# A two-layer decoder trunk in split fp32: the second part of each weight chunk formed by ScalarE and an accumulating transfer

## The chip, the cores and the metric

The kernel runs on one core of a Trainium2 chip. The metric is the device time of one execution in microseconds (us), as the median of several runs. A trace of one profiled execution shows the engines: TensorE (PE, with its weight loads as PEld), VectorE (DVE), ScalarE (ACT), GpSimd (POOL) and the DMA queues of SyncE (SP), ScalarE and GpSimd.

## The reference, cut to what matters

The reference is a decoder trunk of two layers on 512 tokens of width 1024, with 256 memory tokens. What matters here is that nearly all its work is matrix products with weights that are used once:

```python
z = h @ w_in                               # mixers of both layers
return jnp.concatenate([y_a, y_b], axis=-1) @ w_out
q = (h @ w_q).reshape(...)                 # cross-attention, 256 memory tokens
k, v = jnp.split(mem_n @ w_kv, 2, axis=-1)
return o.reshape(b, s, D_MODEL) @ w_o
return jnp.square(jax.nn.relu(h @ w_up)) @ w_down     # MLP, 1024 -> 4096 -> 1024
```

The mixers are a gated linear recurrence beside forgetting attention (layer 0) and dilated beside sliding-window attention (layer 1). Inputs and outputs are fp32.

## The kernel before

Each fp32 operand of a product is split into two parts of the type fp32r: a first part `hi`, the value rounded by ScalarE's copy, and a second part `lo = value - hi`. `mm3` then makes three matmuls of each pair, first part by first part, first by second, and second by first (lines 177, 178 and 179), which add up in one PSUM bank.

Weights come in chunks of 128 x 1024 fp32 (512 KB). There are 246 of them that `chunk` brings in; the first weights of all are loaded apart, in two halves, as `wr_first`. A chunk needs three tiles: `raw` (tag `wr`, **two** buffers), `h` (tag `wh`, three buffers) and `lo` (tag `wl`, three buffers). SyncE loads `raw`, ScalarE writes `h` from it (line 156), VectorE writes `lo` as `raw - h` (line 157). In most stages a chunk then feeds 24 matmuls of 512 columns; a chunk of the cross-attention's key projections feeds 24 of 256 columns.

The order of instructions is the order in which Python emits them, changed by the framework's priorities: `chunk` raises the priority of its instructions by 100, so they stand well ahead of the matmuls that use them in each engine's queue, as far as the buffers allow. Each engine works through its own queue strictly in order; semaphores tie them together. In the mixers, `merge` interleaves the steps of the attention heads with those of the projections by estimated costs and due times.

Names that come up: `kv` and `acth` are work tiles of the MLP (lines 908 and 920: ScalarE takes relu of a PSUM bank and squares it); `rope_raw` in the second layer's mixer sends four transfers of 64 KB per rotated projection through SyncE's queue (line 1009), which swap halves of a tile `kv` inside SBUF; `Stats.add` with `sq=G` has GpSimd square the eight input tiles at the start (line 260); GpSimd also scales the softmax's rows (`p`, line 348). GpSimd issues no transfer in this kernel.

Of the kernel before, what the change touches and what calls it, by code (L numbers as in the profile page):

```python
# [9 lines left out]
F32 = mybir.dt.float32  # L10
F32R = mybir.dt.float32r
BF16 = mybir.dt.bfloat16
AF = mybir.ActivationFunctionType
ALU = mybir.AluOpType
# [22 lines left out]
def build(ctx, tc, a):  # L37
    nc = tc.nc
    V, A, G, T, SY = nc.vector, nc.scalar, nc.gpsimd, nc.tensor, nc.sync
# [113 lines left out]
    def hi_lo(hi, lo, src, scale=None):  # L153

        if scale is None:
            A.activation(out=hi, in_=src, func=AF.Copy)  # L156
            V.tensor_tensor(out=lo, in0=src, in1=hi.bitcast(F32), op=ALU.subtract)  # L157
        else:
            A.activation(out=hi, in_=src, func=AF.Copy, scale=scale)
            V.scalar_tensor_tensor(out=lo, in0=src, scalar=scale, in1=hi.bitcast(F32),  # L160
                                   op0=ALU.mult, op1=ALU.subtract)

    def chunk(src):

        cnt[0] += 1
        i = cnt[0]
        started.append(i)
        with tc.high_priority(100 if len(started) > 4 else 0):
            raw = wp.tile([128, 1024], F32, tag="wr", name=f"wr_{i}", bufs=2)
            h = wp.tile([128, 1024], F32R, tag="wh", name=f"wh_{i}", bufs=3)  # L170
            lo = wp.tile([128, 1024], F32R, tag="wl", name=f"wl_{i}", bufs=3)
            SY.dma_start(out=raw, in_=src)
            hi_lo(h, lo, raw)
        return h, lo

    def mm3(ps, wh, wl, xh, xl, start, stop):
# [4 lines left out]
    def proj(src, xs, after, n=S, ks=range(8), need=(), give=(), bank=None):  # L181


        st = {}

        def f(k):
            def g():
                if not st:
                    st["ps"] = (bank or pmm)()[:, :n]
                    st["w"] = [c.rearrange("p (k m) -> p k m", k=8) for c in (src if type(src) is tuple else chunk(src))]  # L190
                h, lo = st["w"]
                mm3(st["ps"], h[:, k, :], lo[:, k, :], xs[k][0], xs[k][1], k == ks[0], k == ks[-1])
                if k == ks[-1]:
                    after(st["ps"])
            return g

        return [step(0.65 * n / S, f(k), need[k] if len(need) == 8 else need if k == ks[0] else (), give if k == ks[-1] else ()) for k in ks]

    def proj2(src, xs, k0, afters, need=(), banks=None):

        st = {}

        def f(e, k):
            def g():
                if "w" not in st:
                    st["w"] = [c.rearrange("p (e k m) -> p e k m", e=2, k=4) for c in chunk(src)]
                if k == 0:
                    st[e] = (banks[e] if banks else pmm)()
                h, lo = st["w"]
                x = xs[k0 + k]  # L210
                mm3(st[e], h[:, e, k, :], lo[:, e, k, :], x[0], x[1], k == 0, k == 3)
                if k == 3:
                    afters[e](st[e])
            return g

        return [step(0.65, f(e, k), need[k] if need else ()) for e in range(2) for k in range(4)]

    def proj_v(srcs, xs, out, nb, store, give=()):

        st = {}  # L220

        def f(kk, k2):
            def g():
                if not st:
                    st["ps"] = [pmm() for _ in range(min(nb, 3))] + [psc() for _ in range(nb - 3)]
                if k2 == 0:
                    st["w"] = [c.rearrange("p (k m) -> p k m", k=2) for c in chunk(srcs[kk])]
                h, lo = st["w"]
                k = 2 * kk + k2
                for b in range(nb):  # L230
                    c = slice(b * 128, (b + 1) * 128)
                    xh, xl = xs[k][0][:, c], xs[k][1][:, c]
                    T.matmul(st["ps"][b], lhsT=xh, rhs=h[:, k2, :], start=k == 0, stop=False)  # L233
                    T.matmul(st["ps"][b], lhsT=xh, rhs=lo[:, k2, :], start=False, stop=False)  # L234
                    T.matmul(st["ps"][b], lhsT=xl, rhs=h[:, k2, :], start=False, stop=k == 7)  # L235
                if k == 7:
                    for b in range(nb):
                        out.append(store(b, st["ps"][b]))
            return g

        return [step(0.65 * nb, f(kk, k2), (), give if (kk, k2) == (3, 1) else ()) for kk in range(4) for k2 in range(2)]
# [1018 lines left out]
```

## Time and profile before

| what | value |
|---|---|
| median of 3 runs | 1474.03 us (1473.45 to 1474.35) |
| the profiled execution's own time | 1476.31 us |
| span of that execution, from the first to the last instruction | 1474.4 us |
| PE busy | 1441.2 us, 98% of the span |
| DVE busy | 880.9 us, 60% |
| ACT busy | 670.9 us, 45% |
| POOL busy | 162.2 us, 11% |
| chunks formed by `chunk` | 246 |

The busy time of PE is that of overlapping matmuls, so 98% says that PE hardly ever waited, and not that it ran at its peak. The other engines have idle time, which costs nothing as long as what PE needs next is there in time. The difference of 1.9 us between the profiled execution's time and its span lies before the first and after the last instruction.

### The profile page before, as it was taken

Reading aid. Unit: us, or ns where it says so; the run is one execution under the profiler, and the core shown is the slowest. Engines: PE = TensorE matmul, PEld = TensorE weight load, DVE = VectorE, ACT = ScalarE, POOL = GpSimd, SP = SyncE. Lnnn points to the kernel's source line nnn. Section 1 sums busy time; section 2 is a strip of 40 time slices with the busy share of each in tenths; the row PEclk is TensorE's granted clock in tenths of the full one; section 3 lists DMA queues with packets and bytes.
Section 4 is the critical chain, followed back from the end, with each engine's and each line's share of the span. In section 5 each row is a group of like instructions: output and inputs, shape, how many; then the busy total and the mean of one; then the engine's idle time right before and its main releaser. Section 6 shows DMA issues by size and latency. Waiting matters only on the chain.

```text
span 1474.4 us, 18320 instructions
## 1 busy us (share of the span) xinstructions
PE 1441.2 (98%) x6912; PEld 1195.4 (81%) x6912; DVE 880.9 (60%) x1525; ACT 670.9 (45%) x1161; POOL 162.2 (11%) x172
## 2 busy tenths in 40 slices
PE   8999999999999999999999999999999999999996
PEld 5777887888888888888888788788888888888885
DVE  7788876645444444444578989765554444444543
ACT  4777764544431423224457867544444223232342
POOL 3003221001200000000213312300020000000012
PEclk9999999999999999999999999999999999999998
DMA  5222224432233323333332222343333333333331
GB/s 191 83 86 81 78 65 142 133 93 90 86 100 97 94 96 100 100 95 91 100 107 80 79 79 79 100 128 114 88 93 93 99 94 94 100 101 92 96 99 57
DMA packets 46327, 142.83 MB, mean 97 GB/s; under 512 B 5792, under 2 KB 11296, under 8 KB 46240
## 3 DMA queue, kind: packets, MB, share of 16 engines
q1 hardware_dynamic: 45152, 140.63, 31.9%
q8 instruction: 54, 0.88, 0.2%
q10 hardware_dynamic: 1088, 1.05, 0.2%
q14 instruction: 33, 0.27, 0.1%
HBM read 136.15 MB, written 2.10 MB: 94 GB/s over the span
## 4 chain that ended last, share of the span: by engine, by line
PE 84%; DVE 8%; ACT 4%; issue 1%; DMA 1%; SPq 0%; POOL 0%; DVEq 0%; ACTq 0%; POOLq 0%
PE mm L178 24%; PE mm L177 24%; PE mm L179 24%; DVE wl L157 2%; PE t L354 1%; ACT wh L156 1%; PE s L177 1%; PE s L178 1%; PE s L179 1%; PE mm L234 1%; PE mm L233 1%; PE mm L235 1%; DVE hgl L160 1%; PE pv L446 1%; PE s L422 1%
## 5 line engine op out<-in xcount | busy, mean ns | idle before, releaser
L156 ACT ACTIVATE wh<-wr 128x1024 fp32r<-128x1024 f32 x246 | 260.2, 1059 | 560.3 <-PE mm L178 508.2
L157 DVE TENSOR_TENSOR wl<-wr,wh 128x1024 fp32r<-128x1024 f32 x246 | 302.6, 1231 | 245.5 <-ACT wh L156 238.2
L177 PE MATMUL mm<-hgh,wh 128*128 128x512 f32 x888 | 350.7, 395 | 0.9 <-DVE qkl L576 0.7
L178 PE MATMUL mm<-hgl,wh 128*128 128x512 f32 x888 | 347.8, 392 | 3.7 <-DVE hgl L160 3.7
L179 PE MATMUL mm<-hgh,wl 128*128 128x512 f32 x888 | 347.1, 391 | 0.0
L177 PE MATMUL mm<-acth,wh 128*128 128x512 f32 x504 | 197.8, 395 | 0.8 <-DVE hT L474 0.8
L178 PEld LDWEIGHTS mm<-hgl,wh 128*128 128x128 f32 x888 | 167.4, 189 | 36.4 <-DVE hgl L160 4.4
L178 PE MATMUL mm<-actl,wh 128*128 128x512 f32 x504 | 196.7, 390 | 0.1
L179 PE MATMUL mm<-acth,wl 128*128 128x512 f32 x504 | 196.7, 390 | 0.0
L177 PEld LDWEIGHTS mm<-hgh,wh 128*128 128x128 f32 x888 | 167.3, 188 | 34.4 <-DVE qkl L576 1.1
L179 PEld LDWEIGHTS mm<-hgh,wl 128*128 128x128 f32 x888 | 167.2, 188 | 33.9
L270 POOL TENSOR_TENSOR ssq<-ssq,sq 128x512 f32<-128x512 f32 (+1 forms) x48 | 72.4, 1508 | 984.3 <-ACT sq L258 983.9
L934 DVE TENSOR_TENSOR kv<-mm,Rt 128x512 f32<-128x512 f32 x56 | 38.7, 692 | 150.8 <-PE mm L179 150.8
L177 PEld LDWEIGHTS mm<-acth,wh 128*128 128x128 f32 x504 | 94.4, 188 | 20.8 <-ACT acth L156 1.4
L179 PEld LDWEIGHTS mm<-acth,wl 128*128 128x128 f32 x504 | 94.6, 188 | 19.5
L178 PEld LDWEIGHTS mm<-actl,wh 128*128 128x128 f32 x504 | 94.7, 188 | 19.1 <-DVE actl L157 0.7
L348 POOL TENSOR_SCALAR p<-p,den 128x256 f32<-128x256 f32 (+1 forms) x96 | 65.7, 689 | 255.5 <-DVE den L347 186.2
L177 PE MATMUL mm<-v,wh 128*128 128x256 f32 (+1 forms) x260 | 87.0, 335 | 0.0
L178 PE MATMUL mm<-v,wh 128*128 128x256 f32 (+1 forms) x260 | 86.9, 334 | 0.0
L179 PE MATMUL mm<-v,wl 128*128 128x256 f32 (+1 forms) x260 | 86.8, 334 | 0.0
L474 DVE TENSOR_TENSOR hT<-hT,mm 128x512 f32<-128x512 f32 x53 | 35.8, 682 | 52.5 <-PE mm L179 52.4
L157 DVE TENSOR_TENSOR ptl<-t,pth 128x128 fp32r<-128x128 f32 (+3 forms) x112 | 53.2, 482 | 10.0 <-ACT pth L156 9.5
(293 smaller groups left out, 2110.8 us busy)
## 6 DMA issues: line engine op xcount, KB each, us to landing
wr<-in_mlp_up SPq DMA_DIRECT2D x64, 512.0 KB, 3.6
wr<-in_mlp_down SPq DMA_DIRECT2D x64, 512.0 KB, 3.6
wr<-in_cd_w_in SPq DMA_DIRECT2D x18, 512.0 KB, 3.7
wr<-in_xa_q SPq DMA_DIRECT2D x16, 512.0 KB, 3.7
wr<-in_xa_k SPq DMA_DIRECT2D x16, 512.0 KB, 3.7
wr<-in_xa_v SPq DMA_DIRECT2D x16, 512.0 KB, 3.7
wr<-in_xa_w_o SPq DMA_DIRECT2D x16, 512.0 KB, 3.6
wr<-in_ab_w_in SPq DMA_DIRECT2D x15, 512.0 KB, 3.6
```

The lines of the kernel that those rows point to most:

```text
L156: A.activation(out=hi, in_=src, func=AF.Copy)
L157: V.tensor_tensor(out=lo, in0=src, in1=hi.bitcast(F32), op=ALU.subtract)
L160: V.scalar_tensor_tensor(out=lo, in0=src, scalar=scale, in1=hi.bitcast(F32), op0=ALU.mult, op1=ALU.subtract)
L177: T.matmul(ps, lhsT=wh, rhs=xh, start=start, stop=False)
L178: T.matmul(ps, lhsT=wh, rhs=xl, start=False, stop=False)
L179: T.matmul(ps, lhsT=wl, rhs=xh, start=False, stop=stop)
L233: T.matmul(st["ps"][b], lhsT=xh, rhs=h[:, k2, :], start=k == 0, stop=False)
L234: T.matmul(st["ps"][b], lhsT=xh, rhs=lo[:, k2, :], start=False, stop=False)
L270: eng.tensor_tensor(out=self.ssq, in0=self.ssq, in1=q, op=ALU.add)
L348: G.tensor_scalar(out=p, in0=p, scalar1=dens[:, i:i + 1], scalar2=1.0, op0=ALU.mult, op1=ALU.mult)
L474: V.tensor_tensor(out=hT[:, e, :], in0=hT[:, e, :], in1=ps, op=ALU.add)
L934: V.tensor_tensor(out=t, in0=ps, in1=Rt, op=ALU.mult)
```

## The change

In `chunk` the call of `hi_lo` is replaced by three instructions. ScalarE writes `h` as before. ScalarE then writes `-h` into `lo`. GpSimd then issues a transfer of `raw` onto `lo` with an adding operation, so that `lo` ends as `raw - h`. VectorE has no part in it any more. All other splits (`hi_lo` of activations, of the statistics and of `wr_first`) are as before. Tiles and their numbers of buffers are as before.

```diff
@@ -170,7 +170,9 @@
             h = wp.tile([128, 1024], F32R, tag="wh", name=f"wh_{i}", bufs=3)
             lo = wp.tile([128, 1024], F32R, tag="wl", name=f"wl_{i}", bufs=3)
             SY.dma_start(out=raw, in_=src)
-            hi_lo(h, lo, raw)
+            A.activation(out=h, in_=raw, func=AF.Copy)
+            A.activation(out=lo, in_=h.bitcast(F32), func=AF.Copy, scale=-1.0)
+            G.dma_start(out=lo, in_=raw, accum_op=ALU.add)
```

The lines below the change move down by two. The order in which the instructions stand on an engine is shown at three places.

ScalarE's queue in the MLP's up-projection, before: the copy of a chunk (`wh`), then relu (line 908) and square (line 920) of an earlier chunk's result.

```order
L156 ACTIVATE wh_4984<-wr_4983 128x1024
L908 ACTIVATE kv_4899<-mm_4868 128x512
L920 ACTIVATE acth_4901<-kv_4899 128x512
L156 ACTIVATE wh_5022<-wr_5021 128x1024
L908 ACTIVATE kv_4937<-mm_4906 128x512
L920 ACTIVATE acth_4939<-kv_4937 128x512
```

The same queue and place with the change (lines 910 and 922 are relu and square now):

```order
L173 ACTIVATE wh_5157<-wr_5156 128x1024
L910 ACTIVATE kv_5070<-mm_5038 128x512
L174 ACTIVATE wl_5158<-wh_5157 128x1024
L922 ACTIVATE acth_5072<-kv_5070 128x512
L173 ACTIVATE wh_5196<-wr_5195 128x1024
L910 ACTIVATE kv_5109<-mm_5077 128x512
```

The negation stands behind the relu of an earlier chunk, so one 128x512 instruction lies between a chunk's copy and its negation.

GpSimd's queue at the start of the program, before: the squares of the input tiles, then the first `rstd`. The brackets name what an instruction waits for.

```order
L260 TENSOR_TENSOR sq_6_221<-hT 128x512 [waits DMAHW2_49,DVE_49]
L260 TENSOR_TENSOR sq_7_224<-hT 128x512 [waits DMAHW3_49,DVE_49]
L298 TENSOR_TENSOR rstd_343<-sm_341,half_neg 128x4 [waits DVE_49]
L348 TENSOR_SCALAR p_962<-p_962,den_963 128x512 [waits DMAHW7_49,DVE_49]
L348 TENSOR_SCALAR p_962<-p_962,den_963 128x384 [waits DVE_49]
```

The same with the change (the squares are at line 262):

```order
L262 TENSOR_TENSOR sq_6_222<-hT 128x512 [waits DMAHW2_49,DVE_49]
L262 TENSOR_TENSOR sq_7_225<-hT 128x512 [waits DMAHW3_49,DVE_49]
L175 DMA wl_140<-wr_138 128x1024 [waits DMAHW5_49,Activation_49]
L175 DMA wl_260<-wr_258 128x1024 [waits DMAHW6_49,Activation_49]
L175 DMA wl_350<-wr_348 128x1024 [waits DMAHW5_49,PE_49,Activation_49]
```

The adding transfers of the first chunks stand behind the last square, and each waits for its load and for ScalarE.

SyncE's queue in the second layer's mixer, before: the swaps of one projection (line 1009), then loads of weight chunks, which wait for VectorE to have read a raw buffer.

```order
L1009 DMA kv_6192<-kv_6190 32x512 [waits DMAHW5_49]
L172 DMA wr_6432<-in_cd_w_in 128x1024 [waits DMAHW6_49,DVE_49]
L172 DMA wr_6533<-in_cd_w_in 128x1024 [waits DMAHW7_49,DMAHW1_49,DVE_49]
L1009 DMA kv_6263<-kv_6261 32x512 [waits DMAHW0_49,Activation_49]
L1009 DMA kv_6263<-kv_6261 32x512
```

The same with the change; `DMASW` is the completion of a transfer that GpSimd issued:

```order
L1011 DMA kv_6318<-kv_6316 32x512 [waits DMAHW5_49]
L172 DMA wr_6562<-in_cd_w_in 128x1024 [waits DMAHW6_49,DMASW0_49]
L172 DMA wr_6664<-in_cd_w_in 128x1024 [waits DMAHW1_49,DMAHW7_49,DMASW1_49,Activation_49]
L1011 DMA kv_6391<-kv_6389 32x512 [waits DMAHW0_49,DVE_49,Activation_49]
L1011 DMA kv_6391<-kv_6389 32x512
```

The place of the loads among the swaps is the same; each load now waits for an adding transfer to have landed.

## Rows read from the trace of the kernel before

**Rows 1.** The page: busy time by engine, transfers by queue, the two groups replaced.

```profile
PE 1441.2 (98%) x6912; PEld 1195.4 (81%) x6912; DVE 880.9 (60%) x1525; ACT 670.9 (45%) x1161; POOL 162.2 (11%) x172
...
q1 hardware_dynamic: 45152, 140.63, 31.9%
...
L156 ACT ACTIVATE wh<-wr 128x1024 fp32r<-128x1024 f32 x246 | 260.2, 1059 | 560.3 <-PE mm L178 508.2
L157 DVE TENSOR_TENSOR wl<-wr,wh 128x1024 fp32r<-128x1024 f32 x246 | 302.6, 1231 | 245.5 <-ACT wh L156 238.2
```

**Rows 2.** Waits, PE only: waiter, releaser, us in total, times, longest.

```profile
PE mm L177 <- ACT wh_first L156: 5.8, 1, 5.8
PE mm L178 <- DVE hgl L160: 5.0, 3, 2.1
...
PE pv L445 <- DVE kv L395: 0.5, 1, 0.5
PE t L354 <- DVE v L157: 0.4, 1, 0.4
```

**Rows 3.** Timeline, MLP of layer 0, ACT, DVE and SP: start, length, instruction, idle before.

```profile
566.28 1.06 ACT L156 ACTIVATE wh<-wr 128x1024 fp32r<-128x1024 f32 x1 [4.38 <-PE mm L178]
567.25 0.58 ACT L908 ACTIVATE kv<-mm 128x512 f32<-128x512 f32 x1
...
571.72 1.06 ACT L156 ACTIVATE wh<-wr 128x1024 fp32r<-128x1024 f32 x1 [3.23 <-PE mm L178]
...
567.37 1.23 DVE L157 TENSOR_TENSOR wl<-wr,wh 128x1024 fp32r<-128x1024 f32 x1 [3.75 <-ACT wh L156]
...
568.63 0.33 SPq L172 DMA_DIRECT2D wr<-in_mlp_up  x1
```

**Rows 4.** Issues of transfers: size, median us from issue to landing.

```profile
wr<-in_mlp_up SPq DMA_DIRECT2D x64, 512.0 KB, 3.6
...
kv<-kv SPq DMA_DIRECT2D x52, 64.0 KB, 2.0
```

**Rows 5.** Line 172 (the loads) from 262 to 268 us, two loads.

```profile
DMA to landing us min/median/max: 3.5/4.1/4.7
```

**Rows 6.** Stretches; DVE and ACT instructions that read `wr` only (count = chunks).

```profile
core 0: us, DVE busy (x) ACT busy (x), PEclk, DMA share, GB/s
13.00:95.00 82.00, 17.93 (x15) 15.75 (x15) 1.00 0.35 107
95.00:207.00 112.00, 15.73 (x13) 12.62 (x12) 1.00 0.24 74
207.00:293.00 86.00, 24.62 (x20) 21.11 (x20) 0.98 0.42 127
293.00:352.00 59.00, 9.97 (x9) 8.48 (x8) 1.00 0.28 83
352.00:743.00 391.00, 89.15 (x73) 77.38 (x73) 1.00 0.32 97
743.00:933.10 190.10, 25.71 (x22) 23.28 (x22) 1.00 0.28 80
933.10:1016.00 82.90, 25.36 (x20) 20.04 (x19) 1.00 0.45 134
1074.00:1441.00 367.00, 83.08 (x68) 72.26 (x69) 1.00 0.32 96
```

**Rows 7.** Timeline at the start, POOL and DVE.

```profile
22.25 1.96 POOL L260 TENSOR_TENSOR sq<-hT 128x512 f32<-128x512 f32 x1 [0.63 <-DVE ssq L270]
...
19.52 1.21 DVE L157 TENSOR_TENSOR wl<-wr,wh 128x1024 fp32r<-128x1024 f32 x1
```

**Rows 8.** Waits, DVE only, from 743 to 932 us.

```profile
DVE kv L1015 <- DMA kv<-kv: 3.7, 2, 3.2
```

**Rows 9.** The end: a stretch (PEclk after the engines), and PE's timeline.

```profile
1462.00:1474.00 12.00, 2.50 (x10) 2.07 (x9) 5.66 (x13) 0.89 (x2) 3.02 (x4) 0.53 0.51 175
...
1459.36 0.71 PE L308 MATMUL t<-ident,rstd 128*128 128x128 f32 x4 [0.45 <-POOL rstd L298]
1465.76 1.23 PE L308 MATMUL t<-ident,rstd 128*128 128x128 f32 x4 [1.14 <-POOL rstd L298]
```

## The prediction, made before the change was run

> **What bounds the kernel now.** I read the page first: PE is busy 98% of the span, DVE 60%, ACT 45%, POOL 11% [rows 1]. The waits of PE are the next view. There are 18 rows of them, from 5.8 us down to 0.2 us, 25 us in all; twelve name DVE, from 5.0 us to 0.4 us, and these add up to 14.5 us [rows 2]. So what DVE is relieved of can give back 14.5 us at most, and the kernel is bound by PE.
>
> Then the cadence of a chunk. In the MLP, ACT's copy of one chunk starts at 566.28 and of the next at 571.72 us: PE uses up a chunk in 5.44 us, and ACT's copy has idled 4.38 us until PE released a `wh` buffer [rows 3]. Over the program, 508 of the 560 us that ACT idled before these copies ended with PE [rows 1]. The weights therefore come ahead of PE, and the question is how much room there is.
>
> The room is that of the two raw buffers. A raw buffer goes round so: SyncE issues the load, 0.03 us after DVE has read the chunk before (567.37 + 1.23 = 568.60, issue at 568.63); the load lands 3.6 us later; ACT copies it (1.06 us); DVE subtracts (1.23 us) [rows 3, 4]. That is 5.9 us of work; with two buffers a chunk could come every 3.0 us. PE wants one every 5.44 us, so today the loop has 2 x 5.44 = 10.88 us for 5.9 us of work.
>
> **The change part by part.** It takes 246 DVE instructions of 1.231 us away, 302.6 us [rows 1]. DVE is not the bound; of this at most the 14.5 us above come back, and only where DVE is late for another reason than a chunk. I count nothing.
>
> It adds 246 negations on ACT. The trace has none; the nearest row is the copy of the same shape, 1.06 us [rows 3], so between nothing and 1.06 us, and I take 1.06. ACT goes from 671 to some 930 us busy, 63% of the old span [rows 1]. That hides in ACT's 560 us of idle time before the copies; but the negation lies inside the loop of the raw buffer. In the MLP's up-projection a relu of 0.58 us stands between copy and negation (the order above); that is half of the MLP's chunks, so 0.3 us on average.
>
> It adds 246 transfers from SBUF to SBUF that read `raw` and `lo` and write `lo`. The load of the next chunk waits for their landing, and so do the matmuls of line 179. Call the time from the negation's end to the landing D. No row shows an adding transfer, nor any transfer that GpSimd issues. Two rows give a plain transfer: 64 KB inside SBUF lands after 2.0 us, 512 KB from HBM after 3.6 us [rows 4]. A line through them is 1.77 us fixed and 1.83 us per 512 KB. From below, D is 3.6 us, if reading the second operand costs nothing. The middle: two operands are read, 1.77 + 2 x 1.83 = 5.4 us. On top comes the load that runs beside it: the loads keep the 16 DMA engines 31.9% of 1474.4 us for 140.63 MB, which is 268 times 512 KB: 1.75 us per chunk [rows 1]; half of this is 0.9 us. GpSimd makes these transfers in place of SyncE's queue, at a cost between nothing and the 2 us that one of its squares takes; SyncE's own issue, which is part of the landing times above, takes 0.33 us [rows 3, 7], and nearer to that I take 0.5. So D = 5.4 + 0.9 + 0.5 = 6.8 us. From above, if the adding halves the rate of the whole transfer: 2 x 5.4 = 10.8 us. I take the middle because the second read is certain and the halving is not.
>
> The load has the adding transfer beside it too. Two loads that met other traffic landed after 3.5 and 4.7 us, 4.1 on average [rows 5]; I take 4.2 for all.
>
> One round of a raw buffer is then 0.03 + 4.2 + 1.06 + 0.3 + 1.06 + 6.8 + 0.05 (handing over) = 13.5 us, and a chunk comes every **6.75 us**, where PE wants 5.44. All but D is 6.7 us of it, so the room is used up at D = 10.88 - 6.7 = 4.2 us, or at 4.8 us if the loads keep their 3.6.
>
> The sum goes by stretches [rows 6]: the number of chunks times 6.75 us, less the length of the stretch, where that is positive. 13 to 95 us: 15 x 6.75 - 82 = 19. 207 to 293 (cross-attention of layer 0): 135 - 86 = 49. 352 to 743 (MLP): 493 - 391 = 102. 933 to 1016 (cross-attention of layer 1): 128 - 83 = 45. 1074 to 1441 (MLP): 466 - 367 = 99. The mixers' attention (12 chunks in 112 us, 22 in 190) and the output projections (8 in 59, and another such stretch of 58 us) need a chunk every 7.3 us or less often: nothing. Together **314 us**.
>
> Two more terms. At the start, GpSimd's queue holds the squares ahead of the first adding transfer; the last ends at 22.25 + 1.96 = 24.2 us, and D later is 31.0, where DVE had the first `wl` ready at 19.52 + 1.21 = 20.7 [rows 7]: **10 us**. In the second mixer the swaps stand behind loads that wait in SyncE's queue, now for a landing that comes up to 6.8 + 1.06 - 1.23 = 6.6 us later. There are 13 sets of swaps, so between nothing and 86 us; DVE had waited for a swap only twice, 3.7 us in all [rows 8], so they come with time in hand, and I take a quarter, **21 us**. GpSimd's row scaling stands behind adding transfers that wait for ACT. There a chunk is needed every 8 to 9 us only [rows 6], so its load and copy are long done; I count nothing, and if the cover failed, 34 chunks at one negation each, 36 us.
>
> The sum is 314 + 10 + 21 = 345 us on the profiled execution's 1476.3 us: 1821 us. The median of the runs is 2.3 us below that execution, so I predict **1819 us**.
>
> **A rule against it.** The Trainium skill, "DMA: Bandwidth & Descriptors", in its section on the anatomy of a DMA by the GpSimd path, puts such a transfer at about 2.0 us plus its bytes over 436 GB/s. For 512 KB that is an estimate of 3.2 us, with D below the bound at which the loop breaks. By it a chunk would come every 4.65 us, and the sum would be 13 us in the two cross-attention stretches, 7 at the start and 10 for the swaps: some 1504 us. No row here shows this path. The same skill, "Collectives: The Full Stack", in its part on why ReduceScatter is half of AllGather, says that the adding in a transfer costs no time of its own, but that two reads halve the rate; that is the middle value above, from another side.
>
> **The rivals.**
> *The adding transfer is hidden.* With D = 3.6 and loads at 3.6 us a round is 9.7 us, 4.85 per chunk, less than 5.44. Only the cross-attention stretches are denser: 20 x 4.85 - 86 = 11 and 19 x 4.85 - 83 = 9. With 7 at the start and 11 for the swaps: 1512 us. For it: plain transfers of this size [rows 4]. Against: it reads a second operand.
> *The adding is slow.* D = 10.8: 8.75 us per chunk. The sums over all stretches are 732 us, with 14 and 35 beside them: 2255 us. Against it: nothing in the trace; for it: nothing either, it is the upper bound.
> *The clock falls.* At the end, where PE was busy 2.5 of 12 us, the granted clock was 0.53, near the lower of its two levels, 1.2 of 2.4 GHz, and four matmuls took 1.23 us in place of 0.71 [rows 9]. If that met half of the 196 chunks of the stretches that lengthen, each would take 5.44 x 1.73 = 9.4 us: 98 x 2.65 = 260 us more, 2079 us. Against it: PE would still be busy 5.44 of every 6.75 us, far more than at the end.
> *It gets faster.* If D is below 2.8 us, the densest stretch (4.3 us per chunk [rows 6]) is covered too (0.03 + 3.6 + 1.06 + 1.06 + 2.8 + 0.05 = 8.6), and what is left is DVE's relief: 1476.3 + 5.5 at the start - 14.5, or 1465 us in terms of the median. It takes an adding transfer of 512 KB that lands hardly later than a plain one of 64 KB (2.0 us).
>
> **How the numbers follow.** The forecast has a chance of 0.53; its own range, D from 5.4 to 8.4 us, is 1677 to 1988 us by the same sums (6.05 and 7.55 us per chunk). Hidden 0.14, slow adding 0.21, clock 0.08, faster 0.03; 0.01 is left. The range of 1500 to 2160 us takes in the hidden case, the forecast, the clock, and slow adding up to D = 10 us; it leaves out the rest of slow adding and the faster case. All but the last two hundredths or so of these end slower than before by more than 0.2%, about what a measurement of this kernel can tell from no change: faster 0.03, same 0.02, slower 0.95.
>
> **What would show it.** In the profile after, ACT's `wh` waits for the load and no longer for PE; PE waits for the adding transfers' `wl` or for `wh`, in each chunk of the MLP and not in the mixers' attention; the landing of GpSimd's transfers gives D, and the distance of two copies in the MLP gives half a round. DVE falls by some 300 us and ACT rises by some 260. Wrong would be: copies still 5.44 us apart (hidden); a distance near 6.75 but a much longer mixer (queues, not the loop); a granted clock near 0.5 over the MLP; or a D whose length is GpSimd's own issuing time and not the transfer.

## The result, and the profile after

The changed kernel takes 1759.17 us (median; 1743.68 to 1781.21 us over four runs), against 1474.19 us before in the same comparison: a ratio of 1.190, with an interval of 1.182 to 1.197. That is 285 us slower, where 345 were forecast, and inside the range. One of the four runs, the one of 1781.21 us, counts as slow and is not in the ratio; the median of the other three is 1758.37 us.

The page of the changed kernel answers to [rows 1]: busy time by engine, the two groups that now form the second part, the transfers by queue (`q0` is GpSimd's).

```profile
PE 1543.7 (88%) x6912; PEld 1233.7 (70%) x6912; DVE 612.7 (35%) x1279; ACT 900.3 (51%) x1405; POOL 353.6 (20%) x418
...
q0 software_dynamic: 35424, 128.99, 39.9%
q1 hardware_dynamic: 45152, 140.63, 26.9%
...
L173 ACT ACTIVATE wh<-wr 128x1024 fp32r<-128x1024 f32 x246 | 260.0, 1058 | 694.0 <-DMA wr<-in_mlp_down 218.5
L175 POOL DMA_DIRECT2D wl<-wr x246 | 213.8, 870 | 1211.6 <-ACT wl L174 1028.6
...
L174 ACT ACTIVATE wl<-wh 128x1024 fp32r<-128x1024 f32 x246 | 259.1, 1054 | 3.5
```

DVE fell by 268 us and ACT rose by 229, where some 300 and 260 were forecast; neither is near being full. What matters is who releases ACT's copy. Before, it was PE, with 508 of 560 us; now it is the load. PE itself waits for the adding transfer, though not at each chunk as forecast: in the MLP of layer 0 at 26 of 73. The waits of the changed kernel, of ACT and then of PE, which answer to [rows 2]:

```profile
ACT wh L173 <- DMA wr<-in_mlp_down: 218.5, 44, 8.0
ACT wh L173 <- DMA wr<-in_mlp_up: 214.3, 46, 8.7
ACT wh L173 <- PE mm L180: 53.0, 29, 7.0
...
PE mm L181 <- DMA wl<-wr: 97.5, 67, 4.6
PE mm L236 <- DMA wl<-wr: 33.0, 14, 4.6
```

One round of a raw buffer can be read off the timeline in the MLP of layer 0, as in [rows 3]: SyncE's load, ACT's copy and negation with the relu between them, GpSimd's issue, and SyncE's next load into the same buffer.

```profile
692.26 0.33 SPq L172 DMA_DIRECT2D wr<-in_mlp_up  x1
...
696.82 1.06 ACT L173 ACTIVATE wh<-wr 128x1024 fp32r<-128x1024 f32 x1 [3.95 <-DMA wr<-in_mlp_up]
697.78 0.58 ACT L910 ACTIVATE kv<-mm 128x512 f32<-128x512 f32 x1
698.26 1.05 ACT L174 ACTIVATE wl<-wh 128x1024 fp32r<-128x1024 f32 x1
...
699.60 0.86 POOL L175 DMA_DIRECT2D wl<-wr  x1 [6.10 <-ACT wl L174]
...
706.39 0.33 SPq L172 DMA_DIRECT2D wr<-in_mlp_up  x1
```

Load 4.56 us until the copy starts, copy to end of negation 2.49, to GpSimd's issue 0.29, from there to the next load 6.79: 14.1 us, and a chunk every 7.1 us at this place. The landing times of line 172 (loads) and line 175 (adds) from 422 to 902 us, as minimum, median and maximum, in this order:

```profile
DMA to landing us min/median/max: 3.4/4.3/6.3
...
DMA to landing us min/median/max: 4.5/5.5/7.9
```

Where the time went, by the start of ACT's copy of the same chunk in both traces (chunk 1 at 13.2 and 12.9 us, the 16th at 97.6 and 122.2, and so on at the edges of the stretches):

| stretch (chunks) | before | after | longer by | forecast |
|---|---|---|---|---|
| first projections (15) | 84.5 | 109.2 | 24.8 | 19 + 10 |
| attention, layer 0 (12) | 110.0 | 109.9 | -0.1 | 0 |
| cross-attention, layer 0 (20) | 90.7 | 126.8 | 36.1 | 49 |
| its output projection (8) | 54.1 | 62.8 | 8.7 | 0 |
| MLP, layer 0 (73) | 396.3 | 480.2 | 83.9 | 102 |
| attention, layer 1 (22) | 186.5 | 204.8 | 18.3 | 21 |
| cross-attention, layer 1 (19) | 85.0 | 129.4 | 44.4 | 45 |
| its output projection (8) | 54.1 | 61.5 | 7.3 | 0 |
| MLP, layer 1 (68) | 366.5 | 430.6 | 64.1 | 99 |

With 4 us less at the two ends these are the 284 us between the spans (1758.2 and 1474.4).

### The profile page after: what moved, and what is told of

The parts are those of the page before. It is cut to its first block, busy times and chain, and to the rows that moved or that the text cites. A ratio compares the mean times of both kernels' runs of the same rounds, so it can differ in the third digit from the quotient of the medians.

```text
span 1758.2 us, 18948 instructions
## 1 busy us (share of the span) xinstructions
PE 1543.7 (88%) x6912; PEld 1233.7 (70%) x6912; DVE 612.7 (35%) x1279; ACT 900.3 (51%) x1405; POOL 353.6 (20%) x418
## 3 DMA queue, kind: packets, MB, share of 16 engines
q0 software_dynamic: 35424, 128.99, 39.9%
## 5 line engine op out<-in xcount | busy, mean ns | idle before, releaser
L175 POOL DMA_DIRECT2D wl<-wr x246 | 213.8, 870 | 1211.6 <-ACT wl L174 1028.6
L181 PE MATMUL mm<-hgh,wl 128*128 128x512 f32 x888 | 361.5, 408 | 59.3 <-DMA wl<-wr 59.2
L179 PE MATMUL mm<-hgh,wh 128*128 128x512 f32 x888 | 362.2, 408 | 4.7 <-ACT hgh L159 2.4
L180 PE MATMUL mm<-hgl,wh 128*128 128x512 f32 x888 | 357.1, 402 | 0.6 <-DVE hgl L160 0.6
L174 ACT ACTIVATE wl<-wh 128x1024 fp32r<-128x1024 f32 x246 | 259.1, 1054 | 3.5
L179 PEld LDWEIGHTS mm<-hgh,wh 128*128 128x128 f32 x888 | 173.7, 196 | 40.3 <-ACT hgh L159 3.2
L180 PEld LDWEIGHTS mm<-hgl,wh 128*128 128x128 f32 x888 | 173.4, 195 | 36.3 <-DVE hgl L160 1.8
L923 DVE TENSOR_TENSOR kv<-kv 128x512 f32<-128x512 f32 x56 | 38.8, 692 | 312.8 <-ACT acth L922 171.6
L350 POOL TENSOR_SCALAR p<-p,den 128x256 f32<-128x256 f32 (+1 forms) x96 | 57.7, 605 | 109.3 <-DVE den L349 81.5
L160 DVE SCALAR_TENSOR_TENSOR hgl<-hT,par,hgh 128x512 fp32r<-128x512 f32 x48 | 46.7, 981 | 78.9 <-ACT hgh L159 78.6
```

The source lines that it names most:

```text
L174: A.activation(out=lo, in_=h.bitcast(F32), func=AF.Copy, scale=-1.0)
L175: G.dma_start(out=lo, in_=raw, accum_op=ALU.add)
L179: T.matmul(ps, lhsT=wh, rhs=xh, start=start, stop=False)
L180: T.matmul(ps, lhsT=wh, rhs=xl, start=False, stop=False)
L181: T.matmul(ps, lhsT=wl, rhs=xh, start=False, stop=stop)
L350: G.tensor_scalar(out=p, in0=p, scalar1=dens[:, i:i + 1], scalar2=1.0, op0=ALU.mult, op1=ALU.mult)
```

## The experiments

Two theories were to be told apart. The **loop of the raw buffers**: only the round of a raw buffer counts, and only where it is longer than twice what PE takes for a chunk. A **price per add**: each adding transfer costs, by the transfer engines' work, GpSimd's issue or ScalarE's negation, so the loss goes with their number. All ratios are to the kernel before, run beside them. The MLP figures are for the 73 chunks of layer 0, between the copies of the same chunks as in the table.

**Half of the adds, on every other chunk.** The lines are those against the kernel before.

```diff
-            hi_lo(h, lo, raw)
+            if len(started) % 2:
+                A.activation(out=h, in_=raw, func=AF.Copy)
+                A.activation(out=lo, in_=h.bitcast(F32), func=AF.Copy, scale=-1.0)
+                G.dma_start(out=lo, in_=raw, accum_op=ALU.add)
+            else:
+                hi_lo(h, lo, raw)
```

> Every other chunk is formed by the adding transfer, the rest by VectorE as before. Two theories. The raw-buffer loop: the two raw buffers are given out in turn, so one of them carries all the adds and still goes round once per two chunks in some 11.6 to 12.8 us (the traffic is half, so load and landing are a little shorter); a chunk comes every 5.8 to 6.4 us on average, and the time stays at 1620 to 1750 us although half of the adds are gone. A price per add (transfer engines, GpSimd's issue, ScalarE's work, whichever): half of the 285 us, near 1617 us, and the same as with the adds in pairs.

Measured 1557.04 us, 1.055 (1.053 to 1.056). Below the range of either theory: the landing fell from 5.2 to 4.6 us by the median with half of the adds, and a round is shorter than I had counted. The MLP took 410.2 us, 13.9 more than before; a price per add asks for 42. There a chunk came every 5.6 us, and the buffer that carries the adds went round in 11.5 us on average, which is two chunks. The mechanism shows in the waits of ACT. Line 174 is the copy of the chunks with adds, line 156 that of the chunks without:

```profile
ACT wh L156 <- PE mm L183: 140.9, 80, 4.0
ACT wh L174 <- DMA wr<-in_mlp_down: 127.9, 28, 6.8
ACT wh L174 <- DMA wr<-in_mlp_up: 104.8, 21, 6.9
ACT wh L174 <- PE mm L183: 63.6, 19, 8.7
```

One raw buffer carries all the adds and its copies wait mostly for loads; the copies from the other wait for PE, as before the change.

**As many adds, in pairs.** The same with `len(started) % 4 in (1, 2)`.

> The same number of adding transfers as in the alternating kernel, but on two chunks of every four, so that both raw buffers carry them in turn. Raw-buffer loop: a buffer makes one long round (about 12.5 us) and one short one (about 6.5 us) per four chunks, 4.8 us per chunk on average, under the 5.44 us of PE: 1480 to 1530 us. A price per add: the same as the alternating kernel, near 1617 us.

Measured 1541.65 us, 1.044 (1.041 to 1.046). The MLP took 402.2 us, 5.9 more than before, against 13.9 with the adds in turn; that of layer 1 lost 7.3 against 12.4. So the arrangement matters in the direction of the loop, but both are small. The total is above the loop's range, because the other stretches still lost time: 12.4 us in the first projections (24.8 with all the adds), 11.1 and 7.4 in the cross-attentions, 15.2 in the attention of layer 1 (18.3 with all the adds). The waits of ACT show the loop more plainly than the time does. Line 174 is again the copy of the chunks with adds, line 156 that of the chunks without:

```profile
ACT wh L174 <- PE mm L183: 197.1, 85, 7.6
ACT wh L156 <- DMA wr<-in_mlp_up: 101.6, 24, 5.8
ACT wh L156 <- DMA wr<-in_mlp_down: 92.8, 23, 6.0
```

In this arrangement each chunk with an add is followed in its buffer by one without, and it is now the copies without adds that wait for their loads. The wait goes with the buffer that an add held, and not with the chunk that has the add.

**The add reads HBM.**

```diff
-            G.dma_start(out=lo, in_=raw, accum_op=ALU.add)
+            G.dma_start(out=lo, in_=src, accum_op=ALU.add)
```

> The adding transfer reads the chunk a second time from HBM in place of the raw tile, so the raw buffer is free as soon as ScalarE has copied it. All adds, negations and issues stay; the HBM traffic doubles. Raw-buffer loop: the raw round is 4.4 + 1.1 = 5.5 us, half of it per chunk; what is left is the second-part buffers (three), which allow some 10.9 us from PE's release to the landing: 1485 to 1530 us (start and cross-attention). A price per add or the transfer engines' load: 1760 us or more.

Measured 1544.32 us, 1.048 (1.043 to 1.053). This is the sharpest run. All 246 adds are there and land later than in the change; the transfer engines are busier than in any other kernel; and the loss in the MLPs is nearly gone: 5.2 us in each layer, after 83.9 and 64.1. The total lies above the 1530 us of its range, since the first projections still lost 13.7 us and the attention of layer 1 15.2. From 380 to 781 us of this kernel, then its rows of the transfers, and ACT's wait (the columns of the first row are those of [rows 6], with all engines: PE, its weight loads, DVE, ACT, POOL, granted clock, DMA share, GB/s):

```profile
380.00:781.00 401.00, 397.00 (x1759) 328.21 (x1758) 108.01 (x158) 203.05 (x247) 83.58 (x89) 1.00 0.88 192
...
q0 software_dynamic: 35424, 128.99, 50.9%
...
wl<-in_mlp_up POOLq DMA_DIRECT2D x64, 512.0 KB, 6.2
...
ACT wh L173 <- PE mm L180: 441.8, 179, 8.8
```

The engines are busy 0.88 of that stretch, where the changed kernel had 0.71, and PE goes at its old pace. Once the raw buffer is not held by the add, ACT's copy waits for PE again.

**Half tiles.** The raw tile is cut into two of 512 columns with four buffers, the same bytes; load, copy, negation and add are made for each half. The tile of the first weights of all is cut in the same way (not shown).

```diff
-            raw = wp.tile([128, 1024], F32, tag="wr", name=f"wr_{i}", bufs=2)
+            for j in range(2):
+                c = slice(512 * j, 512 * j + 512)
+                raw = wp.tile([128, 512], F32, tag="wr", name=f"wr_{i}_{j}", bufs=4)
...
+                G.dma_start(out=lo[:, c], in_=raw, accum_op=ALU.add)
```

> The same bytes of raw buffers cut in four tiles of half a chunk; load, copy, negation and adding transfer are made per half, so there are twice as many of each. Raw-buffer loop: a half's round is about 3.3 + 0.6 + 0.6 + 0.6 + 0.3 + 4.4 = 9.9 us, four buffers give a chunk every 4.95 us, under PE's 5.44: 1490 to 1540 us. A price per add: at least as slow as the change, 1760 us or more, since the bytes are the same and the issues double.

Measured 1620.71 us, 1.097 (1.092 to 1.101): half of the loss is gone although the issues double, which a price per add forbids, but the time is 80 us above what I had worked out. The adds of 256 KB landed after 4.5 us, hardly sooner than those of 512 KB, and the order had ScalarE copy both halves before it negated the first. How much each of these two adds was not tried.

**No transfer at all: VectorE adds.**

```diff
-            G.dma_start(out=lo, in_=raw, accum_op=ALU.add)
+            V.tensor_tensor(out=lo, in0=raw, in1=lo.bitcast(F32), op=ALU.add)
```

> ScalarE's copy and negation stay, but VectorE adds the raw chunk to the negated one: no transfer by GpSimd at all. Raw-buffer loop: 3.7 + 1.06 + 0.3 + 1.06 + 1.23 and handing over, 7.5 us a round, 3.8 us per chunk, hidden in the MLP; 1474 to 1485 us. If the 246 negations on ScalarE have a price of their own (they stand in its queue among the softmax's instructions, and the second mixer lost 13 to 18 us in every variant so far), 1485 to 1510 us, with 10 us or more of it in the second mixer.

Measured 1488.42 us, 1.009 (1.007 to 1.010). ScalarE's 246 negations cost 13 us by themselves: 7.1 in the first projections, 4.8 in the attention of layer 1 (10 or more were expected there), 1.9 in the attention of layer 0, 1.5 in its output projection, and 1.6 and 1.4 in the MLPs; the cross-attentions were 2.3 and 3.0 us shorter.

**VectorE negates, the add stays.**

```diff
-            A.activation(out=lo, in_=h.bitcast(F32), func=AF.Copy, scale=-1.0)
+            V.tensor_scalar(out=lo, in0=h.bitcast(F32), scalar1=-1.0, scalar2=None, op0=ALU.mult)
```

> VectorE makes the negation, ScalarE the copy alone; the adding transfer stays. Raw-buffer loop: only the relu between copy and negation goes and the negation may be a little shorter, so a round is shorter by 0.3 to 0.8 us: 1715 to 1760 us. If ScalarE's negations were the price, most of the loss would go: under 1550 us.

Measured 1732.40 us, 1.175 (1.172 to 1.178), as the loop has it: VectorE's negation takes 0.7 us in place of 1.06, and no relu stands ahead of it. The MLPs lost 8.0 and 14.1 us less than in the change. But the attentions lost more, 6.4 us in layer 0 and 26.1 in layer 1, where the change lost nothing and 18.3; why was not found.

**A plain transfer by GpSimd, and one on ScalarE's queue.** Both leave the subtraction out, as their expectations say. GpSimd's transfer writes fp32r from fp32, ScalarE's copies fp32.

```diff
-            G.dma_start(out=lo, in_=raw, accum_op=ALU.add)
+            G.dma_start(out=lo, in_=raw)                      # one kernel
+            A.dma_start(out=lo.bitcast(F32), in_=raw)         # the other
```

> The same transfers by GpSimd without the adding, so the second part comes out as the raw chunk (the subtraction is left out). It splits D. If the second operand's read is what makes the adding transfer long, the landing falls by 1 to 2 us, from 5.5 to about 4, the round to 11.3 us, 5.6 per chunk: 1500 to 1600 us. If GpSimd's path is what makes it long (its own issue takes 0.86 us), the landing stays above 5 us and the time near 1740 us.

> The same plain transfers issued on ScalarE's queue, as plain fp32 (the subtraction is left out, and GpSimd has no part). Landing 3.6 to 4.2 us as for the loads, round 10.2 to 10.8 us with ScalarE's issue in it, 5.1 to 5.4 per chunk: 1480 to 1530 us. If the loss came from any second 512 KB per chunk through the transfer engines, it would stay near that of the adding transfers.

Measured 1549.82 us, 1.050 (1.048 to 1.053), by GpSimd, and 1533.18 us, 1.039 (1.037 to 1.040), on ScalarE's queue, 3 us above its range. The MLPs lost 5.0 and 4.7 us in the first and 2.4 and 1.7 in the second. Both are nearly hidden there. What is left is mostly in the two cross-attentions (18.0 and 19.4; 19.4 and 18.7), where chunks are densest, and at the start. The rows of the transfers, first by GpSimd, then on ScalarE's queue:

```profile
q0 software_dynamic: 35424, 128.99, 23.0%
...
wl<-wr POOLq DMA_DIRECT2D x246, 512.0 KB, 3.4
```

```profile
wl<-wr ACTq DMA_DIRECT2D x246, 512.0 KB, 3.3
```

So GpSimd's path lands 0.1 us later than the other, and the adding is the 1.8 us from 3.4 to 5.2 (medians over the program). The engines' work says the same: 23.0% of 1543.6 us over 246 transfers is 1.44 us each, against 39.9% of 1758.2 us, 2.85 us, with the adding. It is 1.98 times as much, which fits two reads in place of one; no run shows the reads themselves.

**The swaps on another queue.** In the second mixer, the rotary swaps are issued on ScalarE's queue, in the changed kernel and, as a control, in the kernel before.

```diff
-                    SY.dma_start(out=swp[b * 32:(b + 1) * 32, :], in_=raw[o * 32:(o + 1) * 32, :])
+                    A.dma_start(out=swp[b * 32:(b + 1) * 32, :], in_=raw[o * 32:(o + 1) * 32, :])
```

> The changed kernel, with the rotary swaps of the second mixer (13 sets of four transfers) issued on ScalarE's queue, so that they stand behind no load that waits for an adding transfer. The prediction's swap term says that the second mixer lost 18 us because swaps stood behind such loads: then that stretch (205 us) falls to some 188 to 193 us and the whole to about 1745. Against it: the kernel that adds from HBM has loads that do not wait for an add, and lost 15 us there all the same; then the stretch stays within 5 us of the changed kernel's, once what the move itself costs is taken from the control run beside it.

> The control: the kernel before with the same move of the swaps to ScalarE's queue. Four issues of about half a microsecond per set stand in ScalarE's queue then; 1474 to 1490 us, all of the difference in the second mixer (187 us before).

Measured 1787.59 us, 1.209 (1.203 to 1.214), and for the control 1478.18 us, 1.002 (1.001 to 1.003). The attention of layer 1 took 216.2 us in the first, 11.4 more than in the changed kernel, while the move itself costs 3.6 us there (the control). That leaves 7.8 us more, beyond the 5 that the second theory allowed. Taking the swaps from behind the waiting loads gave nothing back. How finely this can be read is another matter: the MLP of layer 1, which the move does not touch, lost 84.4 us in this kernel and 64.1 in the changed one; its adds landed there after 6.0 us on average in place of 5.0. Where that comes from is open.

The most direct change to the loop, a third raw buffer, was not run.

## Why the prediction was right, step by step

**The bound and the loop: right.** The room was said to be that of two raw buffers, and the loss to come where a chunk is needed more often than half a round. The waits of ACT's copies went from PE to the loads. Freeing the raw buffer early while leaving every add in place took 215 of the 285 us away (1759 to 1544), and with the adds in pairs the wait moved to the copies without adds. The attention of layer 0, with a chunk every 9 us, lost nothing.

**D: right in its parts, 0.8 us too long.** Forecast 6.8 us: 3.6 for a plain transfer, 1.8 for the second read, 0.9 for the load beside it, 0.5 for GpSimd. Measured, by the medians over the whole program: 3.3 for a plain transfer, 1.8 for the adding (3.4 to 5.2), 0.1 for GpSimd's path and 0.3 from the negation's end to GpSimd's issue, 5.5 us. By the means in the MLP of layer 0 it is 6.0 us (5.7 and 0.3). The 0.9 for the load beside it found no place of its own: the 3.3 and 3.4 us were measured with as many loads beside the transfers already. What adds beside adds can cost is seen in the mean landing in the MLP of layer 0, 4.6 us with every other chunk and 5.7 with all. GpSimd's 0.86 us for an issue lies inside the landing time. The loads were forecast at 4.2 us and landed at 4.2 by the median over the whole program, 4.3 in that stretch.

**The sum by stretches: right in place, high in size.** A chunk came every 6.58 us in the MLP of layer 0 and every 6.33 in that of layer 1, in place of 6.75; the two together lost 148 us of 201 forecast. This is the term that was mis-sized, and with it the total: D was 0.8 us shorter by the means in the first of the two, and about 1.5 shorter in the second, where the adds landed after 5.0 us on average. Some 12 of the 53 us are counting: 391 us were taken for 73 chunks that take 396.3, and 69 chunks for the 68 of layer 1. The cross-attentions lost 81 of 94. Two stretches that were set to nothing, the output projections, lost 8.7 and 7.3: there a chunk is needed every 6.8 us only on average. In the first of them the eight copies start within 36.0 us before the change, 5.1 us apart, and then none for 18.1 us; after it they start within 47.7 us, 6.8 apart. Counting chunks against the length of a stretch misses that.

**The start: right in sum by luck, not in cause.** 24.8 us against 29. But 7.1 us of it is there with no adding transfer at all, from the negations by ScalarE, which I had counted as nothing outside the loop.

**The swaps: the number fits by luck, the mechanism fell.** 21 us were forecast for the attention of layer 1, and it lost 18.3. Yet it lost 15.2 us with adds from HBM, where the loads do not wait for any add, and moving the swaps to another queue made it worse. What the runs lost there: 4.8 us with the negations and no transfer, 3.0 with plain transfers on ScalarE's queue, 8.4 with plain ones by GpSimd, 13.2 to 18.3 with adding ones of whole chunks, and 26.1 where VectorE makes the negation. So the adding transfers have the larger part, and it does not hang on ScalarE's negation; which wait of PE it is was not found. The waits of PE that the profile lists there add up to 11.0 us. PE's own busy time rose as well, from 184.0 to 193.7 us, at a granted clock of 0.98 after 1.00. VectorE waited 19.1 us for the swaps there, against 3.7 before [rows 8] and 11.7 with the swaps moved, so they did come late; that this is what cost the time was tried and not borne out.

**The rivals.** Hidden: no, D is 1.3 to 1.8 us above the 4.2 at which the room is used up; a plain transfer of this size would have been nearly hidden in the MLP, as its rival said. Slow adding: no, D stayed at 5.5 to 6.0 us, far from 10.8. Faster: no. The clock: PE's granted clock was lower, 0.953 on average after 0.995. In the MLP of layer 0, before and after (columns as above):

```profile
352.40:748.70 396.30, 395.53 (x1760) 327.73 (x1759) 191.91 (x233) 134.89 (x174) 25.27 (x16) 1.00 0.33 98
```

```profile
422.00:902.00 480.00, 424.38 (x1760) 337.00 (x1759) 112.12 (x160) 202.44 (x248) 84.21 (x89) 0.96 0.71 160
```

A clock of 0.96 over 480 us takes 19 us of PE's full-speed time away, so it can have cost 19 of the 83.9 us at most, and over the program 75 of the 284 (4.7% of 1758.2 us less 0.5% of 1474.4). It was 1.00 in the same stretch with adds from HBM. And the steps of the loop without PE nearly add up to the distance of the copies: on average load 4.39, copy to the end of the negation 2.35, GpSimd's issue and handing over 0.38, add 5.69, in all 12.8 us, half of which is 6.4 of the 6.58. In the 0.5 us that a landed chunk waits on average for its copy, a slower PE may have a share.

**The rule against it.** The Trainium skill, "DMA: Bandwidth & Descriptors", in its section on the anatomy of a DMA by the GpSimd path, gives an estimate of 3.2 us for 512 KB; this agrees with the plain transfer (3.4 us here) and not with the adding one (5.2). The sum worked out from it has 12 us and not 13 in the cross-attentions, which changes nothing. What the Trainium skill, "Collectives: The Full Stack", says in its part on why ReduceScatter is half of AllGather, that an add costs the second read and no time of its own, agrees: the engines' time is 1.98 times that of the plain transfer.

## What to carry to other kernels

When work is moved off an engine that is not the bound, ask what buffer the new path holds, and for how long: the round of that buffer, divided by the number of buffers, against the time in which the bound engine uses one up. An adding transfer of 512 KB held its source 5.2 us, where VectorE's subtraction had held it 1.2 us, and with two buffers that set the pace; reading the operand from HBM in place of the buffer took 215 of the 285 us away. Judge dense groups of chunks by their own spacing and not by the average of the stretch.

## What was not expected of the hardware

Halving an adding transfer hardly shortened it: 256 KB landed after 4.5 us, 512 KB after 5.2 us, though there were twice as many of the small ones. An adding transfer keeps GpSimd 0.86 us for its issue, 0.54 us if it only copies (63.05 us over 73 adds, and 39.22 us over 73 plain ones, in the MLP of layer 0). The landing of an add depends on what runs beside it, and not on the number of adds alone: by the median 4.6 us with every other chunk, 4.9 with as many in pairs, 5.2 with all. In the changed kernel the mean was 5.7 us in the MLP of layer 0 and 5.0 in that of layer 1, with the same instructions in both; why was not found.
